# A decoder layer on one core: the first stage with a tile for each stream row and a fixed order, earlier query weights, and two edits in the down projection

## The chip, the cores and the metric

One core of a Trainium2 chip runs the whole kernel in one launch. The metric is device time in microseconds (us), the median of the runs shown; lower is better.

## The reference, cut to what matters

Inputs are a stream `x` (1024 tokens by 1024 channels, float32), a memory of 256 tokens, and the weights of one decoder layer:

```
h  = rms_norm(x, norm_mix_pre)
q_d, k_d, v_d, u_p, q_m, gate_logits = split(h @ w_in)
y_attn = rms_norm(diff_attention(q_d, k_d, v_d, lam), subln_g) * 0.8 @ w_attn_branch
y_pool = multiscale_pool(u_p) @ w_pool_branch
k_m, v_m = split(rms_norm(mem, norm_mem) @ w_mem_kv)
y_mem  = softmax(q_m k_m^T / sqrt(128)) v_m @ w_mem_branch          # 4 heads
x = x + rms_norm((sum of sigmoid(gate_b) * y_b) @ w_out, norm_mix_post)
h2 = rms_norm(x, norm_ffn_pre)
g, v = split(causal_conv3(h2 @ w_up))
x = x + rms_norm((gelu(g) * v) @ w_down, norm_ffn_post)
```

`lam` comes from four vectors of 64 numbers by two dot products and exponentials. Results stand to float32 precision.

## The kernel before, in words

Nearly every product is made from three passes in fp32r: each operand is split into a high half (a rounding copy on ScalarE, line 89) and a low half (a subtraction on VectorE, line 90), and `mm3` (lines 98 to 100) adds high x high, high x low and low x high in PSUM. `split` does both halves. A tile framework traces the program, then a planner orders each engine's instructions by its own estimate of when they are ready; each engine then runs its list strictly in that order. `tc.issue_after(ins)` adds an order edge: what the block traces on the engine of `ins` stands behind `ins` on that engine. It adds no wait between engines.

*First stage* (lines 345 to 486). SP issues the loads in the order of the string `ORDER`: `m0`, `m1` are the two tiles of 128 memory rows, `w0` to `w3` the weights of the four key blocks, `w4` to `w7` those of the values, `x0` to `x7` the eight tiles of 128 stream rows, `g` the gain. All are 512 KB in SBUF. Stream and memory rows share six buffers, so later rows wait for the release of earlier ones. TensorE begins with `keep(16)`, transposes of the identity that compute nothing needed, then transposes the memory rows; ScalarE and VectorE scale them into `memt`. Then come the keys (four blocks, line 467, plain float32), two pairs of stream rows, the values (line 479) and two more pairs. `norm_rows` takes a pair: ScalarE squares both rows (line 128) and takes one root (line 133), VectorE makes the reciprocal root and the scaled rows `xn` (line 458), and `transpose_split` (line 163) turns each row in two groups of four transposes into a PSUM tile out of a pool of two, split from there into `hTh` and `hTl`, the transposed normalized stream. The planner alone decides where the turned rows stand between keys and values. At the end of the stage `make_cols` loads the convolution's weights as rows (lines 271 to 274) and turns them to columns; `make_lambda` loads the four vectors (line 286); all these loads are issued on SP after the big ones.

*Query and pool projections* (lines 490 to 600). `query(j, i)` loads and splits a block of query weights (`wsplit`, line 326) and multiplies it with one half of the stream, lines 98 to 100 as `pq`; `pool_in` does the same for the pool channels. `query(0, 0)` and `query(0, 1)` are traced right behind the first stage; its first score product is `pss`. `down_combinations` prepares sums of down weights (line 504).

*Up projection.* Each channel block uses a scheme with seven products of halves in place of eight (`six`: one was made earlier). Its sixth product `rest` is deferred into the next block; the add into `c22` (line 241) reads the PSUM tile that `rest` then uses.

*Down projection* (lines 1396 to 1590). Seven products `product_d` in the order B11, B21, T2, T1, B22, T3, T4, each over six pairs of channel blocks. `prepare(name, i)` loads the weight page `br`, forms the stream operand in place on VectorE where the product needs a difference (line 1472), and splits both into `page`. After a product `evict` copies the PSUM rows on ScalarE (line 1499) or adds on VectorE (line 1501). T4 adds onto the PSUM rows that T3 leaves, so it starts when T3's rows are evicted. T4 runs its first two pairs for all four token rows, then row by row, so that each row can be normalized and stored while the next runs.

Of the kernel before, what the change touches and what calls it, by code (L numbers as in the profile page):

```python
# [15 lines left out]
P = 128  # L16
# [14 lines left out]
PAD = 24  # L31
KEEP = (16, 0, 3)
ORDER = "m0 m1 w0 w1 x0 g x1 w2 x2 w3 x3 w4 x4 x5 w5 x6 w6 x7 w7".split()
C_V = 2048
# [7 lines left out]
def kernel(  # L42
# [150 lines left out]
    def seven(raws, ss, op, gv, late=None):  # L193
# [25 lines left out]
        else:  # L219
            late.append(copy)  # L220

    def six(raws, ss, op, gv, p2, between):

# [16 lines left out]
        product(s3, op, "T3", pa, False)  # L240
        nc.vector.tensor_tensor(out=c22, in0=pa, in1=c21, op=ALU.add)  # L241

# [24 lines left out]
    def make_cols(const):  # L267
        rows = const.tile([48, 4, P], F32, name="rows")
        nc.gpsimd.memset(rows, 0.0)
        for j in range(3):  # L270
            nc.sync.dma_start(out=rows[0:2 * CT, j, :], in_=conv_w[j].rearrange("(a p) -> a p", p=P))
        nc.sync.dma_start(out=rows[0:2 * CT, 3, :], in_=conv_b[0].rearrange("(a p) -> a p", p=P))
        nc.sync.dma_start(out=rows[44:48, 0, :], in_=pool_scale[0].rearrange("(a p) -> a p", p=P))
        nc.sync.dma_start(out=rows[44:45, 1, :], in_=subln_g)
# [8 lines left out]
    def make_lambda(const):  # L283
        lamv = const.tile([P, 4, 64], F32, name="lamv")
        for j, l in enumerate((lambda_q1, lambda_k1, lambda_q2, lambda_k2)):
            nc.sync.dma_start(out=lamv[:, j, :], in_=l[0:1, :].partition_broadcast(P))
        lamp = const.tile([P, 2, 64], F32, name="lamp")
        for j in range(2):
            nc.vector.tensor_tensor(
                out=lamp[:, j, :], in0=lamv[:, 2 * j, :], in1=lamv[:, 2 * j + 1, :], op=ALU.mult)  # L290
        nc.vector.reduce_sum(out=lame, in_=lamp, axis=AX.X)
# [30 lines left out]

    def wsplit(src, shape):

        raw = wst.tile(shape, F32, tag="raw", name="raw", bufs=2)
        nc.sync.dma_start(out=raw, in_=src)
        hi = wst.tile(shape, F32R, tag="wh", name="wh")
        lo = wst.tile(shape, F32R, tag="wl", name="wl")
# [5 lines left out]
    def proj_half(o, wh, wl, i):  # L334
        for k in range(KT):
            mm3(o, wh[:, k, :], wl[:, k, :], hTh[i][:, k, :], hTl[i][:, k, :], k == 0, k == KT - 1)

    with tc.tile_pool(name="kvm", reuse_waits="tile", bufs=1, side="right") as kvp:
        kmh = kvp.tile([P, MH, NM], F32R, name="kmh")
# [4 lines left out]
        with tc.tile_pool(name="pa", reuse_waits="tile", bufs=2, side="right") as pa, \  # L344
# [106 lines left out]

            def norm_rows(names):
                srcs = [xts.pop(n) for n in names]
                xns = [pa.tile([P, D], F32, tag="xn", name="xn", bufs=4) for _ in names]
                rs = rstd_batch(srcs, [bank2(name="junk") for _ in names])
                for n, xt, xn, r in zip(names, srcs, xns, rs):
                    i = int(n[1])
                    nc.vector.scalar_tensor_tensor(out=xn, in0=xt, scalar=r, in1=gp, op0=ALU.mult, op1=ALU.mult)
                    transpose_split(xn, hTh[i // 4], hTl[i // 4], i % 4 * P)


            for j in range(MH):
                w = raws[j].rearrange("p (k c) -> p k c", k=KT)
                pk = pbank((P, NM), "pk")
                for k in range(KT):
                    with tc.issue_after(roots["pe"].ins):
                        nc.tensor.matmul(pk, w[:, k, :], memt[:, k, :], start=(k == 0), stop=(k == KT - 1))
# [3 lines left out]
                if j % 2 == 1:  # L471
                    norm_rows(["x%d" % i for i in range(j - 1, j + 1)])
            pv = [pbank((P, H), "pv%d" % i) for i in range(2)]
            for k2 in range(4):
                w = raws[MH + k2].rearrange("p (k c) -> p k c", k=2)
                for i in range(2):
                    for kk in range(2):
                        k = 2 * k2 + kk
                        nc.tensor.matmul(pv[i], memt[:, k, i * P:(i + 1) * P], w[:, kk, :],
                                         start=(k == 0), stop=(k == KT - 1))  # L480
                if k2 >= 1 and k2 < 3:
                    norm_rows(["x%d" % i for i in range(2 * k2 + 2, 2 * k2 + 4)])
            for i in range(2):
# [11 lines left out]
        with tc.tile_pool(name="xa", reuse_waits="tile", bufs=2, side="right") as xa:  # L495
# [13 lines left out]
            def query(j, i):  # L509
                if i == 0:  # L510
                    qs[j] = (wsplit(chunk(w_in, C_QM + j * P), [P, KT, P])[:2],
                             xa.tile([P, S], F32R, name="qh"), xa.tile([P, S], F32R, name="ql"))
# [7 lines left out]
            def pool_in(g, i):  # L520
                if i == 0:
                    us[g] = wsplit(chunk(w_in, C_U + g * P), [P, KT, P])[:2]
                wh, wl = us[g]
# [49 lines left out]

            query(0, 0)
            query(0, 1)
# [871 lines left out]
    def prepare(name, i):  # L1447
# [169 lines left out]
```

## Time and profile before

| | us |
|---|---|
| median of 3 runs | 1743.37 (1742.37 to 1744.37) |
| the profiled execution, device time | 1743.73 |
| its span, first to last instruction | 1742.0 |
| TensorE busy | 1717.1 |
| VectorE busy | 1240.8 |
| ScalarE busy | 886.0 |
| mean granted TensorE clock | 0.996 |

Engines: PE is TensorE's matmuls, PEld its weight loads, DVE VectorE, ACT ScalarE, POOL GpSimd, SP the sync engine; a q behind the name is the engine's queue. Matmuls are pipelined, so a duration in the profile is longer than the distance of two starts; the distance is what one costs. The granted clock is 1.0 at 2.4 GHz and 0.5 at 1.2 GHz. A landing is the time at which a transfer's completion was seen.

### The profile page before, as it was taken

The numbers are of one execution on the slowest core, as the hardware profiler recorded it, in microseconds if no ns is written. First come the engines' busy times: TensorE is split into PE (matmuls) and PEld (weight loads), VectorE is DVE, ScalarE is ACT, GpSimd is POOL, SyncE is SP. The second block draws the span as 40 slices with busy tenths as digits, with TensorE's granted clock in tenths as the row PEclk, the third lists the DMA queues.
The fourth block names the chain that finished last, engine by engine and source line by source line (L and its number), as shares of the span: only waits on it lengthen the run. The fifth ranks groups of instructions, "written<-read, shape, count | busy, mean of one in ns | idle before, by whom it ended". The sixth has DMA issues, their size and how long they took to land.

```text
span 1742.0 us, 22417 instructions
## 1 busy us (share of the span) xinstructions
PE 1717.1 (99%) x8112; PEld 1424.3 (82%) x8112; DVE 1240.8 (71%) x2043; ACT 886.0 (51%) x1576; POOL 45.4 (3%) x104
## 2 busy tenths in 40 slices
PE   8999999999999999999999999999999999999997
PEld 6788888888788888888888888888888888788886
DVE  5775875665765568888866555848888888878475
ACT  5434554444544367777754344645555555543452
POOL 0000000000000011111110000000000000000000
PEclk9999999999999999999999999999999999999999
DMA  7773544444884585665556571562432332673343
GB/s 259 266 286 130 170 157 146 122 167 150 250 248 169 180 237 174 184 172 154 152 185 229 187 225 49 169 224 91 128 120 92 121 108 74 220 275 103 109 162 117
DMA packets 232803, 294.41 MB, mean 169 GB/s; under 512 B 15865, under 2 KB 161526, under 8 KB 230006
## 3 DMA queue, kind: packets, MB, share of 16 engines
q1 hardware_dynamic: 229158, 285.61, 51.5%
q0 software_dynamic: 3520, 7.38, 1.2%
q8 instruction: 64, 1.05, 0.2%
q14 instruction: 45, 0.37, 0.1%
q10 hardware_dynamic: 16, 0.00, 0.0%
HBM read 201.10 MB, written 85.56 MB: 165 GB/s over the span
## 4 chain that ended last, share of the span: by engine, by line
PE 87%; DVE 5%; DMA 5%; ACT 1%; SPq 1%; issue 1%; DVEq 0%; ACTq 0%
PE pa L98 8%; PE pa L99 8%; PE pa L100 8%; PE pb L99 5%; PE pb L98 5%; PE pb L100 5%; PE pss L985 3%; PE pd L98 2%; PE pd L99 2%; PE pd L100 2%; PE poa L1041 2%; PE pe L99 2%; PE pe L98 2%; PE pe L100 2%; PE pya L99 2%; PE pya L98 2%
## 5 line engine op out<-in xcount | busy, mean ns | idle before, releaser
L89 ACT ACTIVATE wpage<-s 128x512 fp32r<-128x512 f32 x136 | 85.3, 627 | 104.4 <-DVE s L183 36.2
L90 DVE TENSOR_TENSOR wpage<-s,wpage 128x512 fp32r<-128x512 f32 x136 | 92.8, 688 | 45.8 <-ACT wpage L89 45.8
L1389 DVE SCALAR_TENSOR_TENSOR cvt<-gv,cols,cvt 128x1023 f32<-128x1023 f32 x88 | 112.5, 1278 | 15.7 <-ACT cvt L1385 15.7
L989 DVE CUSTOM_DVE_ANT_0 z<-pss,hbias 128x256 f32<-128x256 f32 (+7 forms) x128 | 94.5, 752 | 25.2 <-PE pss L985 24.0
L994 ACT ACTIVATE z<-z,mx 128x256 f32<-128x256 f32 (+7 forms) x128 | 98.8, 773 | 21.2 <-DVE mx L989 21.2
L98 PE MATMUL pa<-T,wpage 128*128 128x512 f32 x264 | 102.9, 390 | 1.7 <-DVE gv L241 1.7
L99 PE MATMUL pa<-T,wpage 128*128 128x512 f32 x264 | 102.9, 390 | 0.0
L100 PE MATMUL pa<-T,wpage 128*128 128x512 f32 x264 | 102.8, 389 | 0.0
L985 PE MATMUL pss<-ks,q 128*128 128x512 f32 (+5 forms) x384 | 86.6, 350 | 1.4 <-DVE mx L989 1.4
L89 ACT ACTIVATE page<-blk 128x1024 fp32r<-128x1024 f32 (+1 forms) x42 | 41.3, 988 | 90.9 <-PE pe L99 50.6
L90 DVE TENSOR_TENSOR page<-blk,page 128x1024 fp32r<-128x1024 f32 (+1 forms) x42 | 47.6, 1132 | 38.7 <-ACT page L89 38.7
L985 PEld LDWEIGHTS pss<-ks,q 128*128 128x128 f32 x384 | 62.9, 189 | 11.1 <-DVE mx L989 6.2
L98 PE MATMUL pd<-page 128*128 128x512 f32 x176 | 69.2, 393 | 2.6 <-ACT row L1499 2.6
L99 PE MATMUL pd<-page 128*128 128x512 f32 x176 | 69.0, 392 | 0.0
L100 PE MATMUL pd<-page 128*128 128x512 f32 x176 | 69.0, 392 | 0.0
L98 PE MATMUL pa<-hT,wpage 128*128 128x512 f32 x168 | 65.6, 390 | 0.1
L99 PE MATMUL pa<-hT,wpage 128*128 128x512 f32 x168 | 65.5, 390 | 0.0
L100 PE MATMUL pa<-hT,wpage 128*128 128x512 f32 x168 | 65.4, 389 | 0.0
L1041 PEld LDWEIGHTS poa<-aT,v 128*128 128x128 f32 x480 | 60.7, 190 | 3.1 <-ACT srow L1061 1.4
L89 ACT ACTIVATE wh<-raw 128x1024 fp32r<-128x1024 f32 (+1 forms) x38 | 33.3, 877 | 58.0 <-issue 17.9
L1041 PE MATMUL poa<-aT,v 128*128 128x256 f32 (+1 forms) x480 | 62.6, 281 | 0.0
L98 PEld LDWEIGHTS pa<-T,wpage 128*128 128x128 f32 x264 | 49.5, 188 | 12.5 <-DVE gv L241 2.1
(422 smaller groups left out, 4991.0 us busy)
## 6 DMA issues: line engine op xcount, KB each, us to landing
q<-q_d SPq DMA_DIRECT2D x64, 256.0 KB, 5.1
wd<-in_w_down_dram SPq DMA_DIRECT2D x22, 512.0 KB, 5.5
tw_d<-wd SPq DMA_DIRECT2D x11, 1024.0 KB, 6.1
rawv<-in_w_up_dram SPq DMA_DIRECT2D x22, 512.0 KB, 5.3
rawu<-in_w_up_dram SPq DMA_DIRECT2D x22, 512.0 KB, 4.0
ff_d<-cvt SPq DMA_DIRECT2D x22, 512.0 KB, 4.4
blk<-ff_d SPq DMA_DIRECT2D x20, 512.0 KB, 6.8
br<-tw_d SPq DMA_DIRECT2D x20, 512.0 KB, 3.7
```

The costliest lines, as they stand in the source:

```text
L89: copy = nc.scalar.activation(out=hi, in_=src, func=AF.Copy)
L90: nc.vector.tensor_tensor(out=lo, in0=src, in1=hi.bitcast(F32), op=ALU.subtract)
L98: nc.tensor.matmul(o, ah, bh, start=first, stop=False, skip_group_check=onto)
L99: nc.tensor.matmul(o, ah, bl, start=False, stop=False, skip_group_check=onto)
L100: return nc.tensor.matmul(o, al, bh, start=False, stop=last, skip_group_check=onto)
L985: last["scores"] = nc.tensor.matmul(pss[:, i * H:i * H + m], q[:, j, c, ts], keys, start=(j == 0), stop=(j == 1))
L989: nc.vector.tensor_tensor_reduce(out=halves(z[:, 0:n]), in0=pss.rearrange("p (a m) -> p a m", a=2)[:, 0:parts, 0:m], in1=halves(biases[h][ ...
L994: nc.scalar.activation(out=z[:, 0:n], in_=z[:, 0:n], func=AF.Exp, scale=-1.0, bias=mx[:, c:c + 1], accum_out=sm if c else sums[:, h, t:t + 1])
L1041: nc.tensor.matmul(po[:, qs], (vh, vl)[i][:, k, :], w[j][:, ws], start=(n == 0), stop=(n == len(terms) - 1))
L1389: nc.vector.scalar_tensor_tensor(out=cv[:, sh:], in0=u[:, 0:S - sh], scalar=w, in1=cv[:, sh:], op0=ALU.mult, op1=ALU.add)
```

## The change

- `ORDER` has the third key weights ahead of x0, some other loads in new places, and at its end `q0` and `u0`: the first block of query weights and of pool weights, loaded by `wload` and handed to `query(0, 0)` and `pool_in(0, 0)`.
- Rows have eight buffers in place of six. The first run of keepers is 10 in place of 16.
- `norm_rows` only makes `xn`; `turn_row` transposes. Keys, values and turned rows are chained on TensorE in the order written.
- The splits of `query(0, 0)` stand behind the last root on ScalarE and on VectorE. `make_lambda`'s products stand behind the last root on VectorE.
- The ten small loads of `make_cols` and `make_lambda` are issued on POOL; the memset of `rows` is VectorE's.
- In the down projection the difference for T3 is formed in B22's `prepare`. The low halves of B11's third pair stand behind the last add into `c22` on VectorE. The high halves of T4's pairs 1 to 5 stand behind the last eviction on ScalarE.

```diff
-KEEP = (16, 0, 3)
-ORDER = "m0 m1 w0 w1 x0 g x1 w2 x2 w3 x3 w4 x4 x5 w5 x6 w6 x7 w7".split()
+KEEP = (10, 0, 3)
+ORDER = "m0 m1 w0 w1 w2 x0 g x1 w3 x2 x3 w4 x4 x5 w5 x6 x7 w6 w7 q0 u0".split()
...
-        nc.vector.tensor_tensor(out=c22, in0=pa, in1=c21, op=ALU.add)
+        marks["c22"] = nc.vector.tensor_tensor(out=c22, in0=pa, in1=c21, op=ALU.add)
...
-        nc.gpsimd.memset(rows, 0.0)
+        nc.vector.memset(rows, 0.0)
         for j in range(3):
-            nc.sync.dma_start(out=rows[0:2 * CT, j, :], in_=conv_w[j].rearrange("(a p) -> a p", p=P))
+            nc.gpsimd.dma_start(out=rows[0:2 * CT, j, :], in_=conv_w[j].rearrange("(a p) -> a p", p=P))
...
-            nc.sync.dma_start(out=lamv[:, j, :], in_=l[0:1, :].partition_broadcast(P))
+            nc.gpsimd.dma_start(out=lamv[:, j, :], in_=l[0:1, :].partition_broadcast(P))
...
+    def wload(src, shape):
         raw = wst.tile(shape, F32, tag="raw", name="raw", bufs=2)
         nc.sync.dma_start(out=raw, in_=src)
+        return raw
...
-                xt = pa.tile([P, D], F32, tag="xt", name="xt", bufs=6)
+                xt = pa.tile([P, D], F32, tag="xt", name="xt", bufs=8)
...
+                elif what in ("q0", "u0"):
+                    ahead[what[0]] = wload(chunk(w_in, C_QM if what == "q0" else C_U), [P, KT, P])
...
+            def turn_row(n):
+                i = int(n[1])
+                with tc.issue_after(roots["pe"].ins):
+                    roots["pe"] = transpose_split(xns.pop(n), hTh[i // 4], hTl[i // 4], i % 4 * P)
...
+            keys(0)
+            keys(1)
+            norm_rows("x0", "x1")
+            keys(2)
+            norm_rows("x2", "x3")
+            for n in "x0", "x1":
+                turn_row(n)
+            keys(3)
+            norm_rows("x4", "x5")
+            for n in "x2", "x3":
+                turn_row(n)
+            values(0)
+            norm_rows("x6", "x7")
+            for k2 in range(1, 4):
+                turn_row("x%d" % (k2 + 3))
+                values(k2)
+            turn_row("x7")
...
-            query(0, 0)
+            with tc.issue_after(roots["last"].ins), tc.issue_after(roots["rstd"].ins):
+                query(0, 0)
...
-                                  ("B22", a12, a12, a11, ALU.subtract), ("T3", a11, a22, a11, ALU.subtract)):
+                                  ("B22", a12, a12, a11, ALU.subtract), ("B22", a11, a22, a11, ALU.subtract)):
...
-        for p, src in ((pb, b), (pa, a)):
-            split(p[:, 0, 0:n], p[:, 1, 0:n], src)
+        first = marks["c22"] if (name, i) == ("B11", 2) else marks["row"] if name == "T4" and i else None
+        with tc.issue_after(first.ins) if first else nullcontext():
+            for p, src in ((pb, b), (pa, a)):
+                split(p[:, 0, 0:n], p[:, 1, 0:n], src)
...
-            nc.scalar.activation(out=o, in_=acc[t], func=AF.Copy)
+            marks["row"] = nc.scalar.activation(out=o, in_=acc[t], func=AF.Copy)
```

## Rows read from the trace of the kernel before

**Rows 1.** Page, part 1: busy us, share of the span, instructions.

```profile
PE 1717.1 (99%) x8112; PEld 1424.3 (82%) x8112; DVE 1240.8 (71%) x2043; ACT 886.0 (51%) x1576; POOL 45.4 (3%) x104
```

**Rows 2.** Page, part 4: shares of the chain that ended last, by engine.

```profile
PE 87%; DVE 5%; DMA 5%; ACT 1%; SPq 1%; issue 1%; DVEq 0%; ACTq 0%
```

**Rows 3.** Waits of TensorE, whole span: total us, times, longest us.

```profile
PE pt L163 <- DVE hTl L90: 4.6, 2, 4.4
PE pd L98 <- ACT row L1499: 2.6, 1, 2.6
...
PE pa L98 <- DVE gv L241: 1.7, 1, 1.7
```

**Rows 4.** Chain of waits, 0 to 90 us: start, duration, what.

```profile
19.66 12.01 DMA rawm<-in_w_mem_kv_dram
...
33.03 6.81 DMA raw<-in_w_in_dram
...
64.80 0.23 PE pq L100
65.03 0.12 PE pss L98
```

**Rows 5.** Waits of ScalarE, 0 to 60 us.

```profile
ACT wh L89 <- DMA raw<-in_w_in_dram: 7.1, 1, 7.1
```

**Rows 6.** Windows: busy us of each engine (instructions), then clock, DMA share, GB/s.

```profile
41.00:48.00 7.00, 4.78 (x12) 3.01 (x13) 5.50 (x11) 6.29 (x12) 0.00 (x0) 0.51 0.27 77
```

**Rows 7.** Timeline of TensorE, 0 to 57 us: start, busy us, instructions [idle before].

```profile
1.86 3.67 PE L387 MATMUL idle<-ident 128*128 128x128 f32 x16 [1.86 <-POOL ident masks.py:199]
...
9.01 2.86 PE L467 MATMUL pk<-memt,rawm 128*128 128x256 f32 x12 [0.46 <-DVE memt L430]
...
22.89 4.48 PE L467 MATMUL pk<-memt,rawm 128*128 128x256 f32 x20
27.21 1.04 PE L163 MATMUL pt<-ident,xn 128*128 128x128 f32 x8
28.08 2.74 PE L479 MATMUL pv<-rawm,memt 128*128 128x512 f32 x6
...
31.80 4.46 PE L479 MATMUL pv<-rawm,memt 128*128 128x512 f32 x10
36.09 1.04 PE L163 MATMUL pt<-ident,xn 128*128 128x128 f32 x8
```

**Rows 8.** Groups by shape, 0 to 66 us: busy us, mean ns, idle before.

```profile
L90 DVE TENSOR_TENSOR hTl<-pt,hTh 128x512 fp32r<-128x512 f32 x16 | 10.4, 685 | 1.2 <-ACT hTh L89 1.1
...
L89 ACT ACTIVATE hTh<-pt 128x512 fp32r<-128x512 f32 x16 | 8.7, 586 | 0.7 <-PE pt L163 0.7
```

**Rows 9.** DMA queues, 29 to 35.9 us: packets, MB, share of 16 engines.

```profile
q1 hardware_dynamic: 583, 0.20, 10.0%
```

**Rows 10.** Chain of waits, 1390 to 1745 us.

```profile
1511.59 5.70 DMA br<-in_w_down_dram
...
1519.62 0.61 DVE gv L241
...
1694.14 6.24 DMA br<-tw_d
...
1702.40 1.47 ACT row L1499 x3
```

**Rows 11.** Windows at the start of the last down product.

```profile
1703.90:1706.90 3.00, 2.99 (x7) 2.40 (x8) 3.00 (x7) 3.00 (x7) 0.00 (x0) 0.52 0.12 49
1701.40:1712.70 11.30, 8.79 (x33) 7.16 (x34) 11.14 (x22) 7.48 (x17) 0.00 (x0) 0.85 0.23 94
```

**Rows 12.** Groups by shape on VectorE, 1690 to 1742 us.

```profile
L90 DVE TENSOR_TENSOR page<-br,page 128x1024 fp32r<-128x1024 f32 x5 | 6.1, 1219 | 0.4 <-ACT page L89 0.4
```

**Rows 13.** Source line 1472: duration ns, first and last start.

```profile
L1472 DVE TENSOR_TENSOR blk<-blk x24: 689/1221/1229, 1545.8 to 1598.1; 128x1024 f32<-128x1024 f32 x20, 128x512 f32<-128x512 f32 x4
```

**Rows 14.** Waits of TensorE, 60 to 1515 us, the largest.

```profile
PE pss L985 <- DVE mx L989: 1.4, 4, 0.5
```

More of the change, by code (lines that the diff above doesn't have):

```diff
@@ L220, in seven @@
             late.append(copy)
+    marks = {}
     def six(raws, ss, op, gv, p2, between):
@@ L268, in make_cols @@
         rows = const.tile([48, 4, P], F32, name="rows")
[L269 removed]
+        nc.vector.memset(rows, 0.0)
         for j in range(3):
[L271 to L274 removed]
+            nc.gpsimd.dma_start(out=rows[0:2 * CT, j, :], in_=conv_w[j].rearrange("(a p) -> a p", p=P))
+        nc.gpsimd.dma_start(out=rows[0:2 * CT, 3, :], in_=conv_b[0].rearrange("(a p) -> a p", p=P))
+        nc.gpsimd.dma_start(out=rows[44:48, 0, :], in_=pool_scale[0].rearrange("(a p) -> a p", p=P))
+        nc.gpsimd.dma_start(out=rows[44:45, 1, :], in_=subln_g)
         pc = bank((P, 4, 48), "pc")
@@ L285, in make_lambda @@
         for j, l in enumerate((lambda_q1, lambda_k1, lambda_q2, lambda_k2)):
-            nc.sync.dma_start(out=lamv[:, j, :], in_=l[0:1, :].partition_broadcast(P))
+            nc.gpsimd.dma_start(out=lamv[:, j, :], in_=l[0:1, :].partition_broadcast(P))
         lamp = const.tile([P, 2, 64], F32, name="lamp")
[L288 to L291, printed above, removed]
+        with tc.issue_after(roots["rstd"].ins):
+            for j in range(2):
+                nc.vector.tensor_tensor(
+                    out=lamp[:, j, :], in0=lamv[:, 2 * j, :], in1=lamv[:, 2 * j + 1, :], op=ALU.mult)
+            nc.vector.reduce_sum(out=lame, in_=lamp, axis=AX.X)
         with tc.issue_after(roots["last"].ins):
@@ L321, with wsplit @@
     bstack = ExitStack()
-    def wsplit(src, shape):
+    def wload(src, shape):
         raw = wst.tile(shape, F32, tag="raw", name="raw", bufs=2)
         nc.sync.dma_start(out=raw, in_=src)
+        return raw
+    def wsplit(src, shape, raw=None):
+        raw = wload(src, shape) if raw is None else raw
         hi = wst.tile(shape, F32R, tag="wh", name="wh")
@@ L336, in proj_half @@
             mm3(o, wh[:, k, :], wl[:, k, :], hTh[i][:, k, :], hTl[i][:, k, :], k == 0, k == KT - 1)
+    ahead = {}
     with tc.tile_pool(name="kvm", reuse_waits="tile", bufs=1, side="right") as kvp:
@@ L450, with norm_rows, keys @@
             nc.scalar.activation(out=rrow, in_=pr, func=AF.Copy)
-            def norm_rows(names):
+            def norm_rows(*names):
                 srcs = [xts.pop(n) for n in names]
-                xns = [pa.tile([P, D], F32, tag="xn", name="xn", bufs=4) for _ in names]
                 rs = rstd_batch(srcs, [bank2(name="junk") for _ in names])
[L456 to L462, printed above, removed]
+                for n, xt, r in zip(names, srcs, rs):
+                    xns[n] = pa.tile([P, D], F32, tag="xn", name="xn", bufs=4)
+                    nc.vector.scalar_tensor_tensor(out=xns[n], in0=xt, scalar=r, in1=gp, op0=ALU.mult, op1=ALU.mult)
+            def turn_row(n):
+                i = int(n[1])
+                with tc.issue_after(roots["pe"].ins):
+                    roots["pe"] = transpose_split(xns.pop(n), hTh[i // 4], hTl[i // 4], i % 4 * P)
+            def keys(j):
                 w = raws[j].rearrange("p (k c) -> p k c", k=KT)
                 pk = pbank((P, NM), "pk")
-                for k in range(KT):
-                    with tc.issue_after(roots["pe"].ins):
-                        nc.tensor.matmul(pk, w[:, k, :], memt[:, k, :], start=(k == 0), stop=(k == KT - 1))
+                with tc.issue_after(roots["pe"].ins):
+                    for k in range(KT):
+                        last = nc.tensor.matmul(pk, w[:, k, :], memt[:, k, :], start=(k == 0), stop=(k == KT - 1))
+                roots["pe"] = last
                 kt = pa.tile([P, NM], F32, tag="kt", name="kt", bufs=2)
@@ L470, with values @@
                 split(kmh[:, j, :], kml[:, j, :], kt)
[L471 to L474, printed above, removed]
+            pv = []
+            def values(k2):
+                if k2 == 0:
+                    pv.extend(pbank((P, H), "pv%d" % i) for i in range(2))
                 w = raws[MH + k2].rearrange("p (k c) -> p k c", k=2)
[L476 to L482, printed above, removed]
+                with tc.issue_after(roots["pe"].ins):
+                    for i in range(2):
+                        for kk in range(2):
+                            k = 2 * k2 + kk
+                            last = nc.tensor.matmul(pv[i], memt[:, k, i * P:(i + 1) * P], w[:, kk, :],
+                                                    start=(k == 0), stop=(k == KT - 1))
+                roots["pe"] = last
+            xns = {}
+            keys(0)
[15 more added lines that the diff above has]
+            turn_row("x7")
             for i in range(2):
@@ L510, in query @@
                 if i == 0:
-                    qs[j] = (wsplit(chunk(w_in, C_QM + j * P), [P, KT, P])[:2],
+                    qs[j] = (wsplit(chunk(w_in, C_QM + j * P), [P, KT, P], ahead.pop("q", None))[:2],
                              xa.tile([P, S], F32R, name="qh"), xa.tile([P, S], F32R, name="ql"))
@@ L521, in pool_in @@
                 if i == 0:
-                    us[g] = wsplit(chunk(w_in, C_U + g * P), [P, KT, P])[:2]
+                    us[g] = wsplit(chunk(w_in, C_U + g * P), [P, KT, P], ahead.pop("u", None))[:2]
                 wh, wl = us[g]
```

## The prediction

> **What bounds the kernel now.** I read the busy shares first, then the chain of waits, then TensorE's waits, and only then the two stretches that the diff touches. TensorE is counted busy for 99% of the span [rows 1], and 87% of the chain that ended last is its own work [rows 2]. So only time in which TensorE waits or runs slowly can be won. The list of its waits is short [rows 3]: 4.6 us before transposes in the first stage, 2.6 us before the last down product, 1.7 us before the last product of the up projection. All three places are in the diff. Between 60 and 1515 us no wait is larger than a 1.4 us total [rows 14], so the middle offers nothing, and can only lose.
>
> The profiled execution took 1743.73 us with a span of 1742.0, so 1.7 us lie around the span; it is 0.4 us above the median of the timed runs. The sum below is made against 1743.73. About 0.2% (3.5 us) is what a measurement of this kernel can tell from no change.
>
> *First stage.* The key products start at 9.01 us [rows 7], and the first score product of the memory attention, which ends the stage for TensorE, stands at 65.03 us in the chain [rows 4]: 56.0 us. What TensorE has to do in it, by the spacing of starts [rows 7]: 64 key instructions, 20 of them in 27.21 - 22.89 = 4.32 us, so 0.216 each, 13.8 us; 32 value instructions, 10 in 36.09 - 31.80 = 4.29 us, so 0.429 each, 13.7 us; eight rows of eight transposes, 28.08 - 27.21 = 0.87 us a row, 7.0 us; 48 query instructions at 0.23 [rows 4], 11.0 us. Together 45.5 us. The other 10.5 us are loss. Its root is on ScalarE: it waited 7.1 us, once, for the query weights [rows 5], whose load was issued at 33.03 us and took 6.81 us [rows 4], though the key and value weights had all landed at 19.66 + 12.01 = 31.67 us [rows 4]. Behind that wait stood the squares and the evictions of the fifth stream row and those after it; so TensorE stopped for 4.4 us [rows 3], and from 41 to 48 us its granted clock averaged 0.51, that is 1.2 GHz [rows 6]. It did 4.8 us of work in these 7 us, which at 2.4 GHz is half: 2.4 us more. The remaining 3.7 us (10.5 - 4.4 - 2.4) are short waits and small transposes.
>
> **The change part by part.** *Query and pool weights sooner.* Two loads join the end of the list on SP, right behind the value weights. 19 loads had landed by 31.67 us, some 1.6 us each, so they land near 33.3 and 35 us. The 7.1 us wait goes, and with the order set behind the last root the split can't stand ahead of the squares any more. Gain 4.4 + 2.4 = 6.8 us, which is also the upper bound of this edit.
>
> *Fixed order on TensorE.* Turning rows is now chained with the keys and values, and the first two pairs are turned back to back. Only two PSUM tiles serve the transposes, so the second row of a pair waits for one eviction on ScalarE (0.586 us) and one on VectorE (0.685 us) [rows 8], with handover about 1.3 us: 2.6 us for two pairs. Before, the planner put key products there. The four later rows have a value product of 8 x 0.429 = 3.4 us between them, which hides 2 x (0.586 + 0.685) = 2.5 us. Behind a waiting transpose stand all later keys and values, and everything waits for them. I take 2.6 us lost; bounds 0 (evictions ready) and 6.8 (the one such wait seen, with its slow clock).
>
> *Order of the loads, more buffers, fewer keepers.* x0 and x1 move back by one place, 1.6 us each, but the turn is asked for later, behind the third key product, 16 x 0.216 = 3.5 us on; that hides it. Eight buffers let every row's load be issued without waiting for a release; they stay in sequence on SP and only that sequence sets their arrival. Six fewer keepers at 3.67 / 16 = 0.23 us [rows 7] take 1.4 us off TensorE's start; of it at most 1.4 and at least 0 reach the keys, because the second memory row must land first. I take 0.6.
>
> *Ten small loads from SP to POOL, a memset from POOL to VectorE.* POOL has nothing else to do here and VectorE nothing before the first memory products, so issue costs nothing; if the loads held up the identity on POOL's queue, the 1.4 us above would go. Their transfers are the cost. Between 29 and 35.9 us hardly anything else moved, and 583 packets took 10.0% of 16 engines [rows 9]: 0.10 x 6.9 = 0.7 us. Before, they ran behind the big loads; now beside them, so the rows land up to 0.7 us later. I take 0.7, bounds 0 and 0.7. The Trainium skill, "DMA: Bandwidth & Descriptors", section "Queues, rings and completion order", speaks against this move: each DMA engine goes round robin between the queues that have work, a packet at a time, so the new queue doesn't stand back for the loads. By that rule the sum carries these 0.7 us, without it nothing; the trace of before has them on one queue and can't show which.
>
> First stage: 6.8 + 0.6 - 2.6 - 0.7 = 4.1 us, and of the 3.7 us of short waits about half belong to turns that the planner placed behind a late norm; giving back 1.7 us of these I take 5.8 us (bounds -1 and 10).
>
> *The last up product before the third page.* VectorE's add that frees the PSUM half of the last product ended at 1520.23 us; it stood behind the low half of a page, which stood behind ScalarE's page, which waited 5.70 us for a weight load [rows 10]. With the add ordered first, only its own 0.61 us follow the product before it, and TensorE has first instructions of the down projection to run meanwhile. The 1.7 us wait [rows 3] goes, with some 0.2 us of drain: 1.9 us (bounds 0 and 2). The page's low half comes later by one add, 0.61 us; its product is three pages on, so nothing waits.
>
> *Pages of the last product behind the evictions.* ScalarE stood in a page whose weights landed at 1694.14 + 6.24 = 1700.38 us, so three evictions ended only at 1703.87 [rows 10]; TensorE waited 2.6 us [rows 3] and then ran 7 instructions in 3.0 us at a granted clock of 0.52 [rows 11], where 0.23 each are 1.6: 1.4 us more. Evictions straight after each block leave perhaps 0.3 us. Gain 2.6 + 1.4 - 0.3 = 3.7 us. Against it: two pages that VectorE had split before the end of the sixth product now follow it, 4 x 1.2 = 4.9 us [rows 12] on top of a stretch from 1701.4 to 1712.7 in which it was busy 11.1 of 11.3 us [rows 11]. That puts the last page near 1701 + 2 + 11.3 + 4.9 - 0.7 = 1718.5, the last page being second to last in line; TensorE asks for it after 48 + 18 instructions, 66 x 0.23 = 15.2 us, near 1716.6. So up to 1.9 us come back; I take 1.3. Net 2.4 us (bounds 0 and 3.7).
>
> *Sixth product's operands made with the fifth's.* Same 24 subtractions, and they already ran between 1545.8 and 1598.1 us [rows 13], a hundred us before the sixth product. 0.
>
> Sum: 5.8 + 1.9 + 2.4 = 10.1 us; 1743.73 - 10.1 = **1733.6 us**.
>
> **The rivals.** *A, forecast:* 1733.6, own range 1728 to 1737. Chance 0.60.
> *B, the fixed order costs what the early weights give.* One turn waits as long as before and the clock falls once: 6.8 us gone, 1733.6 + 6.8 = 1740.4. For it: VectorE has norms, keys and evictions of all rows to do in the same time, and it is what the transposes waited for [rows 3]. Against: the wait that made it late is removed at its root. Chance 0.12.
> *C, the last product's feed is late by more than the stall that it replaced.* Gain 0 there: 1736.0. For: VectorE busy 11.1 of 11.3 us. Chance 0.13.
> *D, the planner places the middle otherwise* and its waits, now 1.4 us or less each, take up the gain: about 1742. Chance 0.08.
> *E, slower.* Two turns in the fixed order wait for rows that land late, each 4.4 us with 2.4 us of slow clock: 13.6 us, 1747.2. It decides against the change once such waits exceed 10.1 us in all. For: everything is now in one queue. Against: all 21 loads are issued in one row, at 1.6 us each, against 3.4 us of TensorE work per value product. Chance 0.07.
>
> **How the numbers follow.** Range 1728 to 1740: its low end has the first stage near its upper bound, its high end reaches into B; outside lie D, E, most of B's upper half. Below 1739.9 is faster by over 0.2%: A, C and a little under half of B and D: 0.81. Same: 0.12. Slower: 0.07.
>
> **What would show it.** The first score product at 58 to 60 us in place of 65.03; no wait of ScalarE for query weights; no stretch of half clock after 8 us; transposes waiting for the second row's evictions, 1 to 1.5 us, twice. TensorE not waiting near 1511 us; at the start of the last product a wait below 0.6 us with the clock at 1.0; perhaps a wait for a page some 11 to 15 us later. Wrong would be a first stage that ends after 63 us, or new waits of several us between 60 and 1500.

## The result, and the profile after

The changed kernel takes 1746.08 us (median of 22 runs, 1743.65 to 1749.82) against 1743.34 us for the kernel before on the same chip: ratio 1.0016, 95% interval 1.0009 to 1.0023. That is 0.16% slower, inside the 0.2% that the prediction calls no change; forecast were 1733.6 us and a chance of 0.81 for faster. The profiled execution took 1744.45 us with a span of 1742.7.

How many us later each piece of TensorE's work begins than in the kernel before (differences of first starts in the two timelines; the last column is the start of the last matmul; the chain of [rows 4] has the first score product of before at 65.03, the timeline at 64.87):

```
                    first    gate    attention  output   first     second    last
                    score    product branch     product  down pr.  down pr.  matmul
before, start       64.87    610.71  918.47     1005.51  1516.83   1551.50   1735.08
after              +4.76    +6.10    +5.93      +5.94    +5.45     +4.04     +0.57
```

The first stage ends 4.8 us later where 5.8 us sooner was forecast; the middle adds some 1 us; the two places at the end give 4.9 us back (forecast 4.3). The profiled execution lies 1.6 us below the kernel's median; where a median run loses those 1.6 us no trace shows.

The page's busy shares of the changed kernel answer to [rows 1]: TensorE 1.1 us less busy in a span 0.7 us longer.

```profile
PE 1716.0 (98%) x8106; PEld 1423.0 (82%) x8106; DVE 1242.1 (71%) x2044; ACT 887.0 (51%) x1576; POOL 50.4 (3%) x113
```

TensorE's waits in the changed kernel, whole span, as in [rows 3] (total us, times, longest us):

```profile
PE pt L163 <- DVE hTl L90: 6.2, 2, 4.5
PE pk L479 <- DVE kt L482: 3.0, 1, 3.0
PE idle L397 <- POOL ident masks.py:199: 2.5, 1, 2.5
...
PE pk L479 <- DVE sb L117: 1.4, 1, 1.4
...
PE pa L98 <- ACT wpage L89: 1.0, 1, 1.0
...
PE pd L98 <- ACT row L1538: 0.5, 1, 0.5
PE pa L98 <- DVE gv L243: 0.3, 1, 0.3
```

The last two lines are the places mended: 2.6 became 0.5 and 1.7 became 0.3 us. The lines above them are new or larger: the transposes of the first stage wait 6.2 us instead of 4.6, a key product 3.0 us for VectorE's product of an earlier key block with the root row (`rrow`, the memory rows' reciprocal roots laid out as a row, which ScalarE copies out of PSUM), and the middle has gained a wait of 1.0 us (between 450 and 615 us). TensorE's timeline answers to [rows 7]; it shows where the first stage's waits stand:

```profile
9.78 2.83 PE L479 MATMUL pk<-memt,rawm 128*128 128x256 f32 x12 [1.40 <-DVE sb L117]
...
20.16 5.41 PE L479 MATMUL pk<-memt,rawm 128*128 128x256 f32 x16 [3.00 <-DVE kt L482]
25.40 1.04 PE L163 MATMUL pt<-ident,xn 128*128 128x128 f32 x8
30.89 1.77 PE L163 MATMUL pt<-ident,xn 128*128 128x128 f32 x8 [4.46 <-DVE hTl L90]
32.46 4.66 PE L479 MATMUL pk<-memt,rawm 128*128 128x256 f32 x16
...
39.76 1.26 PE L163 MATMUL pt<-ident,xn 128*128 128x128 f32 x8 [1.77 <-DVE hTl L90]
40.85 3.60 PE L495 MATMUL pv<-rawm,memt 128*128 128x512 f32 x8
...
69.63 0.28 PE L98 MATMUL pss<-kmh,qh 128*128 128x256 f32 x1
```

The third key block waits, x1's turn waits, x3's turn waits; from 40.85 us to the first score product TensorE runs without a gap, as the forecast wanted for the whole stage. Windows of the changed kernel beside [rows 6] and [rows 11] (busy us of each engine, then granted clock, DMA share, GB/s):

```profile
20.30:23.70 3.40, 3.40 (x10) 2.78 (x11) 3.33 (x7) 0.38 (x2) 0.00 (x0) 0.59 1.05 404
30.50:34.00 3.50, 3.11 (x12) 2.77 (x13) 2.08 (x5) 3.15 (x7) 0.00 (x0) 0.59 1.14 322
41.00:48.00 7.00, 7.00 (x24) 3.54 (x23) 6.50 (x14) 5.47 (x9) 0.00 (x0) 1.00 0.00 0
...
1703.90:1706.90 3.00, 2.50 (x12) 1.74 (x11) 1.61 (x3) 2.24 (x5) 0.00 (x0) 1.00 1.05 400
```

The slow clock at 41 to 48 us and at 1703.9 us is gone; it now stands behind the two long waits. The chain of waits of the first stage beside [rows 4] tells where they come from (start, duration, what):

```profile
2.75 5.03 SPq L364
7.83 1.61 SPq L358
...
9.96 8.16 DMA xt<-in_x_dram
18.22 1.15 ACT junk L128 x2
19.37 0.28 ACT rrow L460
19.68 0.42 DVE kt L482
...
23.57 1.15 ACT junk L128 x2
...
27.42 1.28 DVE xn L467
...
29.04 1.20 DVE xn L467
30.23 0.61 DVE hTl L90
30.89 1.77 PE pt L163 x8
```

Read from the top. SyncE stood 5 us on one load (2.74 us before), so x0's load was issued at 7.83 us instead of 2.75. ScalarE's square of x1 therefore ran at 18.22 us instead of 13.73; behind it on ScalarE's list stood the copy of the root row, for which the third key block waited. In the kernel before the copy stood in the same place, at 14.79 us, and no key product waited for it. Then the squares of x2 and x3 and VectorE's two norms of the same pair (27.42 and 29.04 us) stood ahead of the low half of x0's eviction (30.23 us), for which x1's turn waited. ScalarE has no wait for the query weights any more [rows 5].

### The profile page after: what moved, and what is told of

Its sections match the earlier page's. It is cut to its first block, busy times and chain, and to the rows that moved or that the text cites. A ratio compares the mean times of both kernels' runs of the same rounds, so it can differ in the third digit from the quotient of the medians.

```text
span 1742.7 us, 22419 instructions
## 1 busy us (share of the span) xinstructions
PE 1716.0 (98%) x8106; PEld 1423.0 (82%) x8106; DVE 1242.1 (71%) x2044; ACT 887.0 (51%) x1576; POOL 50.4 (3%) x113
## 4 chain that ended last, share of the span: by engine, by line
PE 88%; DVE 6%; DMA 3%; ACT 1%; SPq 1%; issue 1%; DVEq 0%; ACTq 0%
PE pa L98 8%; PE pa L99 8%; PE pa L100 8%; PE pb L98 5%; PE pb L99 5%; PE pb L100 5%; PE pss L1021 3%; PE pd L99 2%; PE pd L98 2%; PE pd L100 2%; PE poa L1077 2%; PE pe L99 2%; PE pe L98 2%; PE pe L100 2%; PE pout L99 2%; PE pout L100 2%
```

## The experiments

### Ten small loads on POOL's queue

DMA queues from 0 to 12 us (packets, MB, share of 16 engines), after:

```profile
q1 hardware_dynamic: 3190, 2.53, 75.2%
q0 software_dynamic: 261, 0.16, 16.2%
```

and before:

```profile
q1 hardware_dynamic: 2792, 3.63, 88.8%
```

261 packets, 0.16 MB together, took 16.2% of 16 engines in 12 us, 1.9 us of all of them, and SP's queue moved 1.1 MB less, two of the big loads. From 5 to 6 us it was worst (the two shares make 110%, so the times counted for packets overlap):

```profile
q0 software_dynamic: 15, 0.02, 85.2%
q1 hardware_dynamic: 86, 0.06, 25.2%
```

The first test puts only these loads back on SP; the orders of TensorE, VectorE and ScalarE stay. The second keeps them on POOL and moves the third key weights behind x1.

```diff
-            nc.gpsimd.dma_start(out=rows[0:2 * CT, j, :], ...)
+            nc.sync.dma_start(out=rows[0:2 * CT, j, :], ...)     # and so for all ten
```
```diff
-ORDER = "m0 m1 w0 w1 w2 x0 g x1 w3 x2 x3 w4 x4 x5 w5 x6 x7 w6 w7 q0 u0".split()
+ORDER = "m0 m1 w0 w1 x0 g x1 w2 w3 x2 x3 w4 x4 x5 w5 x6 x7 w6 w7 q0 u0".split()
```

> The changed kernel, with its ten small loads back on SP's queue; the order on TensorE, VectorE and ScalarE is the same as in the changed kernel. Theory P (packets of POOL's queue hold the DMA engines from 4 to 6 us and starve the first big loads): key products start at 8.4 to 9.0 us instead of 9.78, ScalarE takes x0 near 12.5 us instead of 15.39, the first score product moves from 69.6 to 66 or 67 us, and the run is some 3 us faster than the changed kernel. Theory Q (three key weight loads in a row block SP's issue): no move of x0 by more than 0.5 us, the first score product stays at 69 to 70 us.

> The changed kernel, with the third key weights asked for behind x1 as before; POOL keeps the small loads, and apart from which key block is third the engines' orders are the same. Theory Q: ScalarE takes x0 near 12 us instead of 15.39, SP issues it near 3 us instead of 7.83. Theory P: SP's issue still stands still until 7 or 8 us, and x0 comes earlier only by its one place, 1.6 us, near 13.8 us; the first score product near 68 us.

With the loads on SP: 1743.60 us, ratio to the kernel before 0.9999 (0.9988 to 1.0010); x0's square at 12.50 instead of 15.39 us, first score product at 67.41 instead of 69.63: 2.2 us. With the third key weights later, 1743.32 us in one run; x0's square at 13.70 us and the first score product at 67.96, as theory P had them, and SyncE stood as long, now on x0's own load:

```profile
2.76 5.03 SPq L358
```

So it isn't a third load of key weights that stops SP, it is the loads on POOL; that their packets do it by holding the DMA engines is what the queues from 5 to 6 us suggest. That one place of the third key weights is worth 1.7 us here all the same (69.63 against 67.96). And x1's turn waited longer with the loads back on SP:

```profile
17.11 3.72 PE L479 MATMUL pk<-memt,rawm 128*128 128x256 f32 x16 [1.98 <-DVE kt L482]
20.67 1.04 PE L163 MATMUL pt<-ident,xn 128*128 128x128 f32 x8
27.85 1.97 PE L163 MATMUL pt<-ident,xn 128*128 128x128 f32 x8 [6.14 <-DVE hTl L90]
```

The longer wait is not a larger loss: TensorE comes to x1's turn 4.7 us sooner there, and the turn itself runs at 27.85 instead of 30.89 us, when x0's eviction is done. Of the miss of 10.6 us in the first stage, POOL's queue is 2.2; the rest lies elsewhere. These steps come from one profiled execution each, and are good to about 1 us: a kernel with the same orders as the changed one (left operands moved by 256 bytes, below) was profiled with its first score product at 70.69 instead of 69.63 us.

### One part of the change alone

The kernel before with the three edits of the up and down products; the kernel before with the early query weights and the query split behind the roots; and both, the first stage in the planner's free order.

```diff
-        nc.vector.tensor_tensor(out=c22, in0=pa, in1=c21, op=ALU.add)
+        marks["c22"] = nc.vector.tensor_tensor(out=c22, in0=pa, in1=c21, op=ALU.add)
...
-        for p, src in ((pb, b), (pa, a)):
-            split(p[:, 0, 0:n], p[:, 1, 0:n], src)
+        first = marks["c22"] if (name, i) == ("B11", 2) else marks["row"] if name == "T4" and i else None
+        with tc.issue_after(first.ins) if first else nullcontext():
+            for p, src in ((pb, b), (pa, a)):
+                split(p[:, 0, 0:n], p[:, 1, 0:n], src)
```
```diff
-... x6 w6 x7 w7"
+... x6 w6 x7 w7 q0 u0"
...
-            query(0, 0)
+            with tc.issue_after(roots["last"].ins), tc.issue_after(roots["rstd"].ins):
+                query(0, 0)
```

> The kernel before, with only the three edits in the up and down projection (order of the last add, of the last product's pages, operands of the sixth product). Theory: these gain all that the prediction gave them and their gain was eaten by the first stage: TensorE's waits of 1.7 and 2.6 us fall below 0.6 each, no half clock near 1704 us, and the run is 4.3 to 5.5 us faster than before. Rival: the gain in the changed kernel came from a different placing of the middle, and alone they give 2 us or less.

> The kernel before, with only the early query and pool weights and the order of the first query split behind the last roots. Theory: the prediction's first term was right and the fixed order spent it: ScalarE no longer waits 7.1 us, the first score product moves from 64.9 to 58 to 60 us, and the run is 5 to 7 us faster than before. Rival: the planner's free order fills the place with other waits; first score product at 62 us or later, under 3 us gained.

> The kernel before with the early query and pool weights and the three edits in the up and down projection, and the planner's free order in the first stage. Theory: what the early weights gained up to the first score product (4.1 us) was lost again at the two later places that the down edits mend (waits of 2.4 and 3.7 us), so together they add up: first score product at 60.8 us, no wait above 0.6 us near 1513 or 1700 us, the run 7 to 9 us faster than before. Rival: the early weights' gain is lost anywhere behind, and the run is no better than the down edits alone, 4 us faster.

```
us                      first score   first down pr.    second    last matmul   median
before                  64.87         1516.83           1551.50   1735.08       1742.9
up/down edits alone     64.30         1518.25           1551.10   1731.20       1739.13 (0.9959 to 0.9983)
query weights alone     60.79         1514.76           1551.57   1736.54       1742.65 (0.9984 to 1.0005)
both, free order        61.27         1514.88           1547.69   1727.79       1736.84 (0.9956 to 0.9979)
```

All three gained less than expected: 3.7 us (4.3 to 5.5 expected), 0.2 (5 to 7) and 6.0 (7 to 9). From the first down product to the second the edits alone take 1.8 us less time than before, from there to the last matmul 3.5 us less. The query weights alone bring 4.1 us to the first score product, and lose them in the profiled execution: 2.0 us between the first score product and the first down product (with no one cause traced; the edits alone and both together lose 1.7 to 2.0 us there too), 2.1 from there to the second and 1.4 from the second to the last matmul, where the same two waits take more than before. That execution, 1745.37 us, is among the slowest of its 12, so a median run loses less. TensorE's waits at the two places, query weights alone:

```profile
PE pd L98 <- ACT row L1508: 3.7, 1, 3.7
PE pa L98 <- DVE gv L241: 2.4, 1, 2.4
```

against the up/down edits alone:

```profile
PE pa L98 <- ACT wpage L89: 0.8, 1, 0.8
...
PE pd L98 <- ACT row L1503: 0.5, 1, 0.5
```

Both together, without the written order, are 6.0 us faster than the kernel before (0.9956 to 0.9979), and no stretch of slow clock is left up to the first score product. So the loss sits in the parts that this version leaves out: the written order with its order of loads, buffers and keepers, and POOL.

### What the written order waits for

All three stand on the version with the loads on SP: the norm of each pair written behind the turns of the pair before it; the copy of the root row ahead of the squares on ScalarE; both.

```diff
             keys(2)
-            norm_rows("x2", "x3")
             for n in "x0", "x1":
                 turn_row(n)
+            norm_rows("x2", "x3")
```
```diff
-            nc.scalar.activation(out=rrow, in_=pr, func=AF.Copy)
+            roots["rrow"] = nc.scalar.activation(out=rrow, in_=pr, func=AF.Copy)
...
+                with tc.issue_after(roots["rrow"].ins):
+                    rs = rstd_batch(srcs, [bank2(name="junk") for _ in names])
```

> The changed kernel with the small loads on SP, and each pair's norm traced behind the turns of the pair before it, so that VectorE evicts the first turned row ahead of the next pair's scaled rows. Theory (the second row of a pair waits because VectorE's list has the next pair's norm in front of the first row's eviction): the wait of 6.1 us before a transpose falls to about 1.5 us, the half clock goes, and the first score product moves from 67.4 to 60 to 62 us. Rival: only two PSUM tiles serve the turns, so the wait stays above 4 us.

> The changed kernel with the small loads on SP, and ScalarE's copy of the memory's root row ordered ahead of the squares of the stream rows. Theory: the keys' products wait for their PSUM tile because the copy stands behind squares that wait for x1; the 2.0 us wait before the third key block goes, VectorE's list changes with it, and the first score product moves from 67.4 to 63 to 65.5 us. Rival: the wait only moves to the turn of x1; 67 us.

> The changed kernel with the small loads on SP, the copy of the root row ahead of the squares, and each norm traced behind the turns of the pair before. Theory: with the three causes away the fixed order gives what was predicted: first score product at 58 to 61 us, the run 8 to 11 us faster than before. Rival: the chain costs by itself; first score product above 63 us, under 6 us gained.

The root row first: third key block without a wait, first score product at 63.51 (3.9 us sooner than with the loads on SP alone), 1739.15 us in one run. TensorE's key blocks and x1's turn there:

```profile
11.13 7.50 PE L480 MATMUL pk<-memt,rawm 128*128 128x256 f32 x34
...
24.10 1.97 PE L163 MATMUL pt<-ident,xn 128*128 128x128 f32 x8 [4.53 <-DVE hTl L90]
```

The norms written later moved little, 1742.58 us in one run, first score product at 66.72, with x1's turn still waiting 4.9 us; both together took 1740.54 us (0.9974 to 0.9992), first score product at 64.10, no better than the root row alone and what the rival of the third expectation said. ScalarE's timeline of that last version says why:

```profile
20.83 1.03 ACT L128 ACTIVATE junk<-xt 128x1024 f32<-128x1024 f32 x1 [0.82 <-DVE xn L468]
...
21.89 1.01 ACT L128 ACTIVATE junk<-xt 128x1024 f32<-128x1024 f32 x1
...
23.23 1.06 ACT L89 ACTIVATE hTh<-pt 128x512 fp32r<-128x512 f32 x2
```

Written later or not, the planner put the squares of x2 and x3 ahead of x0's eviction, and the first of them waits for x1's norm: the statistics tile has two buffers, and the memory rows hold one until the stage ends.

### More buffers for the statistics

```diff
-        st = small.tile([P, 5, m], F32, tag="sb%d" % m, name="sb", bufs={1: 4, 2: 2, 4: 1}[m])
+        st = small.tile([P, 5, m], F32, tag="sb%d" % m, name="sb", bufs={1: 4, 2: 4, 4: 1}[m])
...
-            st = small.tile([P, 5, 2], F32, tag="sb2", name="sb", bufs=2)
+            st = small.tile([P, 5, 2], F32, tag="sb2", name="sb", bufs=4)
```

> The changed kernel with one size changed: the tile of the row statistics (squares' sums, roots) has four buffers instead of two. One of the two is held by the memory rows' own statistics until the stage's end, so all pairs of stream rows shared the other, and the squares of x2 and x3 stood 3.0 us on ScalarE, ahead of the evictions of the turned x0, until x0's and x1's norms had been applied. The ten small loads stay on POOL's queue. Theory S (that shared buffer makes the 4.5 us wait of x1's turn): the wait falls to 1.8 us or less (the wait of x3's turn was 1.77), the half clock of 30.5 to 34 us goes, the first score product begins at 65 to 67 us instead of 69.6, the median falls by 2.5 to 4 us, to some 1742.5. Rival W (ScalarE is simply full there: eight evictions, keys and squares of about 1 us each): the wait stays over 3.5 us wherever the squares stand, first score product 68.5 to 70, median 1745 to 1746.

> The changed kernel with all three mends of the first stage: the ten small loads back on SP, the copy of the root row ahead of the squares on ScalarE, and four buffers for the statistics. Theory S: the turn of x1 no longer waits 4.53 us (as it did with the first two mends) but 1.8 or less, no half clock between 10 and 60 us, first score product at 59 to 61 us instead of 63.5, median 1735 to 1737. Rival W: wait over 3.5 us, half clock of 5 to 7 us stays, first score product 63 to 64.5, median 1739 to 1740.5.

> The kernel before with the early query weights and the three edits of the products, in the planner's own order (the fastest so far, 1736.84), and four buffers for the statistics. Theory S: the buffer costs only where turns stand back to back in a written order; the planner's order puts keys or values between them, so little is left: first score product 60 to 61.3 us (61.27), median 1735.5 to 1737. Rival: the shared buffer set the pace of the planner's order too: 58 to 59.5 us, median 1733.5 to 1735. The planner places the middle anew, worth up to 2 us either way.

All three medians missed: 1747.11, 1748.98 and 1740.99 us (1.0005 to 1.0022, 1.0014 to 1.0036, 0.9977 to 0.9998). On the chip of these three the kernel before took 1744.51 us, 1.2 us more than beside the changed kernel (1743.34) and 1.7 more than beside the fastest version so far (1742.85); without that part the misses stand, but are smaller. In the first, the stage did what was expected: x1's turn waited 2.46 instead of 4.46 us, no slow clock behind it, first score product at 65.37. In the second the planner used the buffers to put the squares of x2, x3, x4 and x5 all ahead of x0's eviction (24.18 us), and the turn waited 5.15 us; there the theory fell: the buffer permits the order, it doesn't make it. And every one of them lost some 5 us in three products that the edit doesn't touch: pb from yph at 222 us, the attention branch's at 918 us, the output's at 1005 us. In the first of the three kernels TensorE's instructions and their order are those of the changed kernel. TensorE's groups, the attention branch's product in that kernel (busy us, mean ns):

```profile
L98 PE MATMUL pya<-ath,wh 128*128 128x512 f32 x128 | 50.6, 395 | 0.0
```

and in the changed kernel:

```profile
L98 PE MATMUL pya<-ath,wh 128*128 128x512 f32 x128 | 49.8, 389 | 0.0
```

### Where the operands lie

Two buffers more moved all that lies on the left of the memory by 128 bytes of each partition (by the compiled program, wh from 28288 to 28416); ath, on the right, stayed at 155520. So: an unused tile of 128 or of 256 bytes on the left and nothing else; then the statistics freed without moving anything, the memory rows' own statistics taking part of the padding tile on the right, in the changed kernel and in the fastest version so far.

```diff
+    lpad = ctx.enter_context(tc.tile_pool(name="lpad", bufs=1, side="left"))
+    lpad.tile([P, 32], F32, name="lpad")          # 64 for 256 bytes
```
```diff
-PAD = 24
+PAD = 8
...
-            st = small.tile([P, 5, 2], F32, tag="sb2", name="sb", bufs=2)
+            st = pad.tile([P, 5, 2], F32, name="sm")
```

> The changed kernel with an unused tile of 128 bytes of each partition on the left of the memory; every engine's instructions stay as they are. Theory A (the place of the left operands against the right ones sets the matmul's time there): the attention branch's product takes 393 to 395 ns a matmul instead of 389, the two products behind it too, the first score product stays at 69 to 70 us, and the kernel is 4 to 6 us slower, some 1751. Rival O (the new order on ScalarE and VectorE in the run with four buffers did it): 389 ns, 1745 to 1747.

> The same with 256 bytes. Theory A with a place that repeats every 256 bytes (left and right operands then stand to each other as before): 389 ns, 1745 to 1747. Theory A with a longer repeat: 391 to 395 ns, 1748 to 1752. Rival O: 389 ns.

> The changed kernel; the memory rows' statistics lie in a part of the padding tile on the right, so that the pairs of stream rows have both buffers of their tag, and nothing else moves. With theory S and theory A both: x1's turn waits 2 to 3 us instead of 4.46, no half clock at 30.5 to 34 us, first score product at 65 to 66 us instead of 69.6, the attention branch's matmuls 389 ns, median 1741 to 1743. If what the first stage gives is lost to something else than the placing: 1745 to 1747.

> The early query weights and the three edits of the products in the planner's order, with the statistics apart as in the run before. By the same two theories: the 5 us that four buffers cost here (1741.0 against 1736.8) come back; first score product 60.5 to 61.5 us, matmuls of the attention branch 389 ns, median 1735 to 1737.5.

```
us                                   matmul of attention branch   median     interval of the ratio
changed kernel                       389 ns                       1746.08    1.0009 to 1.0023
changed, left moved by 128 bytes     395 ns                       1751.46    1.0036 to 1.0061
changed, left moved by 256 bytes     389 ns                       1746.02    1.0009 to 1.0028
changed, statistics apart            389 ns                       1743.12    0.9991 to 1.0009
query weights + up/down, stat. apart 389 ns                       1735.60    0.9947 to 0.9972
```

The attention branch's product with 128 bytes:

```profile
L100 PE MATMUL pya<-ath,wh 128*128 128x512 f32 x128 | 50.6, 395 | 0.0
```

The place alone costs 5.4 us at 128 bytes and nothing at 256: shown (one of the three products lies ahead of the attention branch, at 222 us, not behind it as my expectation has it). By the starts in the timeline a matmul of the attention branch costs 0.2333 us instead of 0.2267. The output's product shows that it is the place of one operand against the other: its stream operand lies on the left, its weights half on the left (`woa`) and half on the right (`wo`); of the 48 matmuls of a token row the first 24, with both operands moved, cost 0.229 us against 0.228, the last 24, with one moved, 0.233 against 0.227. The 768 matmuls with one operand on either side account for 5.0 of the 5.4 us. With equal places the freed statistics bring 2.9 us in the changed kernel (1743.12 us, against 1746.02 with 256 bytes on the same chip; 1746.08 for the changed kernel itself). The profiled execution of that run, at 1746.81 us among the slowest of its 11, doesn't show them: SyncE stood 5.9 us instead of 5.0, x0's square came at 17.21 us, and x1's turn waited 4.4 us, so my numbers for its trace failed while its median held; that the median's gain is the shorter wait is likely from the trace with four buffers (2.46 us), not shown. With POOL's loads in, SyncE stood 4.5 to 5.9 us in all six profiles. The last row is the fastest version run, 7.3 us below the kernel before, first score product at 60.12.

## Why the prediction was wrong, step by step

**Early query weights, 6.8 us: right in kind, too large.** The wait of ScalarE and the slow clock at 41 to 48 us went, as said; alone the edit brought 4.1 us. What I took too large is the wait: turned rows waited 6.1 us in all before (4.6 for evictions, 1.5 for norms) and still 4.0 with the edit (2.0 and 2.0), so that 2.1 us of waits went, not 4.4, beside the 2.4 of slow clock. The forecast's further 1.7 us of short waits, given back, didn't come: the wait for norms grew. One reading was off without touching the sum: behind ScalarE's wait stood the squares of the seventh and eighth rows, not those of the fifth, and the evictions from the fifth on.

**POOL's loads, 0.7 us: the mis-sized term.** I priced their packets as they ran on SP's queue [rows 9]: 0.10 x 6.9 x 16 / 583 = 0.019 us of one engine each. On POOL's queue 261 packets took 0.162 x 12 x 16 / 261 = 0.12 us each as the profile counts them, and at the start of the kernel, when x0's load was late by whatever went ahead of it. Measured: 2.2 us. The step "issue costs nothing" failed too: a load now issued at 1.35 us stands ahead of the identity on POOL, whose wait is 2.5 us instead of 1.86 [rows 7]. The rule of the Trainium skill that the prediction weighed ("DMA: Bandwidth & Descriptors", section "Queues, rings and completion order") is that an engine takes its queues in turn, a packet at a time. The trace agrees in direction: SP's queue moved 1.1 MB less in 12 us beside POOL's. By the rule alone a packet has no price, and the price was what was missing.

**Order of the loads, 0: the step that failed most.** "The turn is asked for later; that hides it" looked at TensorE alone. The squares of x0 and x1 came 4.6 and 4.5 us later (x0's still 1.7 with the loads on SP), and ScalarE's list has the copy of the root row behind them, for which the third key block waited 3.0 us: 3.9 us by the run that turned these two round. This copy has no term in the sum.

**Fixed order, 2.6 us lost.** I took a second turn to wait for one eviction, 1.3 us. x3's turn waited 1.77, near that; x1's 4.46 (4.2 to 6.1 in the variants with the loads on SP), since next pair's squares and norms stand ahead of the eviction. From the start of the keys to the first score product the written order with its loads takes 63.51 - 7.79 = 55.7 us with both other faults mended. Before it took 55.9, of which the early weights alone bring 4.1: so the order costs some 3.9 us, where I took 2.6. Order of turns and order of loads weren't parted in it.

**Fewer keepers, 0.6.** With the loads on SP the keys start at 7.76 us, 1.25 sooner; with POOL's, 0.77 later.

**The up and down products, 1.9 and 2.4 us: right, the second larger.** Alone 1.8 and 3.5 us. (The 5.70 us that I gave as ScalarE's wait for a page is the whole transfer; ScalarE waited 3.6. No term used it.) The late page of the last product, for which I gave 1.3 us back, never came: TensorE waits 0.5 us before that product and nowhere in it after, though VectorE's share looked full. **Operands of the sixth product, 0**: no wait for them appears.

**Rivals.** What came is B's mechanism, one turn that waits as long as before with a slow clock behind it (4.46 us, and 1740.54 us with the other two faults mended beside B's 1740.4; I gave it 0.12), and on top of it two losses that no rival had: the copy of the root row and the price of POOL's packets. E, at 0.07, has nearly the time, 1747.2, and late rows, but its two turns that wait for rows didn't come: one wait was a key block's for the copy, the other a turn's for an eviction. That its time is near is luck. My reason against it, loads at 1.6 us each, took their pace from a row in which nothing else shared the engines. D happened in small, 1.0 us of wait in the middle; why that page came late isn't traced.

Walked from the measured steps: 4.1 (weights) - 3.9 (order) + 1.2 (keys sooner) = 1.4 us gained at the first score product, as in the run with loads and root row mended; - 3.9 (root row) - 2.2 (POOL) = 4.7 lost, 4.8 in the trace after. The steps are differences along one row of runs, so that they close is bookkeeping and no further proof; the order's 3.9 is what is left over.

## What to carry to other kernels

An order written for one engine is only as good as the lists of the engines that feed it: before fixing TensorE's order, read on ScalarE's and VectorE's timelines what stands ahead of each eviction and each small copy that it will wait for, and what happens to that list when the loads come later. Price a transfer that changes queues by packets of the new queue, at the place where it will run. And when a buffer is added, compare the matmul's mean duration in stages that the edit doesn't touch.

## What the runs showed of the hardware

- The first POOL loads of small rows cost far more engine time a packet than SP's: 15 packets counted for 85.2% of 16 engines in one us (counted times overlap there), while SP's queue and they moved 81 GB/s together where the kernel before moved 315.
- A shift of 128 bytes of the left operands against the right ones made the same matmuls 395 ns instead of 389 (128x128 by 512, in the attention branch's product; in two others 6 ns in the pooled product and 3 on the mean of the output's, all of it in the half with one operand moved), 5.4 us in all; a shift of 256 bytes made no difference. Places in between, and why it is so, weren't tried.
- A gain ahead of a stage can be lost behind it: 4.1 us sooner at 60 us, 2.0 of it gone by the first down product, and the waits near 1515 and 1705 us grew from 1.7 and 2.6 to 2.4 and 3.7 us. From 1517 to 1521 us the granted clock was 0.71 (1.00 in the kernel before), from 1705 to 1708 us 0.74 (0.71 before).
